# Second mixer: the groups merged inside the attention, the last projection tile by tile, the FFN begun on two of four token tiles

## Chip, cores and metric

One core of a Trainium2 chip runs the whole kernel. The metric is the device time of one execution in microseconds; the runs of the kernel before took 1180.83 to 1183.24, with a median of 1181.82. The chip's times come with one profiled execution, whose rows are quoted below.

## What is computed

A two-layer decoder trunk on 512 tokens of width 1024 in fp32. Each layer has a mixer and a gated FFN with a causal depthwise convolution, each between two RMS norms. The change touches the end of the second (odd) mixer and the start of both FFNs.

```python
def odd_mixer(h, w_in, w_out):
    cq, ck, cv, sq, sk, sv = split_cols(h @ w_in, ODD_SPLITS)
    o_dil = dilated_attention(groups(cq), groups(ck), groups(cv), slopes)  # 3 groups (window, dilation)
    o_sb = stick_breaking_attention(...)                                   # 4 heads
    return concatenate([heads_last(o_dil), heads_last(o_sb)], -1) @ w_out  # 512 x 1024
# dilated_attention, per block of 128 queries: each group g gives o_g and its log of the softmax sum;
#   wts = softmax over the groups of those logs;  o = sum over g of wts[g] * o_g
# one layer:
h = odd_mixer(rms_norm(x, pre_g), w_in, w_out);  x = x + rms_norm(h, post_g)
h = conv_ffn(rms_norm(x, ffn_pre_g), ...);       x = x + rms_norm(h, ffn_post_g)
# conv_ffn: u = causal_dwconv(h @ w_up); gate, up = split(u); (silu(gate) * up) @ w_down
```

## The kernel before

Tokens lie in four tiles of 128 (`X[0]` to `X[3]`), worked in the order `ORDER = (3, 2, 1, 0)`. The activations for the next product are held turned, 128 features by 512 tokens for each of eight feature blocks, as a high part `xh` and a low part `xl` (float32r). Every fp32 product is three float32r products, `mm3` (lines 249 to 251): high by high, high by low, low by high. Weights come through `Weights`: a load of 512 KB on SP into one of three `wraw` buffers, a cast on ScalarE (`wh`, line 71) and a subtraction on VectorE (`wl`, line 72), a few units ahead of use.

PSUM has eight banks in named groups: `BANKS = {"a": 3, "s": 2, "t": 1, "o": 1, "n": 1}`. A tile that takes a bank waits until the one that had it before has been read. The order of each engine's instructions is set when the program is built, by a scheduler that works from the order in the code and from its own estimates; within `tc.manual_schedule(engines=...)` the engines named keep the order of the code. At run time each engine works its own queue strictly in that order.

The end of the second mixer. The stick-breaking output `oS` is ready early. The dilated attention keeps two sets of results: groups 1 and 2 together (`on`, with their softmax sums in column 64 and minima in column 65; gathered by 16 small DMAs, line 1089) and group 0, worked tile by tile as score, turn (transposes), value, in `score0`, `turn0` and `value0`, with tiles of the value projection (`apv`) between them. `value0` copies its bank to `o0`. When all tiles are through, the merge weights `wt` are worked out for all tiles at once (lines 1160 to 1169). Then, for each tile, `merge(i)` weighs and adds the two results, transposes them (bank `t`) and splits them into `oh` and `ol`; `project(i, 0)` multiplies the S part of a tile (12 products with `oS`), `project(i, 1)` the merged part (12 products). The S part of a tile stands before the merged part of the tile ahead of it. `residual` follows (mean square in two halves on ScalarE, gain on VectorE, `rstd` on GpSimd, then `X` at line 238), then `normalise` (mean square of `X`, line 187, `rstd`, gain at line 200), and its `turn` (eight transposes in two groups of four at line 206, and two splits) is put off by a tile.

The FFN's first four blocks of u (`u4`, 128 features by 512 tokens each) are made specially, since the last tile is normalised late: first tokens 128 to 511 (`rest`), feature block by feature block, with the pending turn at `k == TURN`; then the last tile's 128 tokens with the weights as the moving operand (`ur`, 512 columns), copied to `us` by ScalarE and transposed into `u4` (line 367). All later blocks take 512 columns at once. This code serves both layers; the first mixer leaves one turn pending, and so does the second.

## Time and profile before

| | |
|---|---|
| median of the runs | 1181.82 us |
| profiled execution, its own time | 1183.89 us |
| its span, first to last instruction | 1182.1 us |
| TensorE busy | 1153.9 us, 98% |
| VectorE, ScalarE, GpSimd busy | 808.9, 556.7, 57.2 us |
| first product of the second mixer's projection | at 786.77 us |
| first product of the second FFN (u) | at 825.19 us |
| first u product of 512 columns there | at 850.79 us |

In rows of a timeline the columns are start, duration, engine, line, operation, result and operands, shape, count; in brackets the idle time of the engine before it and what ended it. [...] In rows of windows the columns are the stretch and its length, then the busy time of PE, PEld (weight loads), DVE, ACT and POOL, the granted TensorE clock (1.00 is full speed), the share of the DMA engines and GB/s.

### The profile page before, as it was taken

Reading aid. Unit: us, or ns where it says so; the run is one execution under the profiler, and the core shown is the slowest. Engines: PE = TensorE matmul, PEld = TensorE weight load, DVE = VectorE, ACT = ScalarE, POOL = GpSimd, SP = SyncE. Lnnn points to the kernel's source line nnn. Section 1 sums busy time; section 2 is a strip of 40 time slices with the busy share of each in tenths; the row PEclk is TensorE's granted clock in tenths of the full one; section 3 lists DMA queues with packets and bytes.
Section 4 is the critical chain, followed back from the end, with each engine's and each line's share of the span. In section 5 each row is a group of like instructions: output and inputs, shape, how many; then the busy total and the mean of one; then the engine's idle time right before and its main releaser. Section 6 shows DMA issues by size and latency. Waiting matters only on the chain. (4 is left out here: it accounts for less than half of the span.)

```text
span 1182.1 us, 14868 instructions
## 1 busy us (share of the span) xinstructions
PE 1153.9 (98%) x5520; PEld 939.7 (79%) x5520; DVE 808.9 (68%) x1401; ACT 556.7 (47%) x937; POOL 57.2 (5%) x139
## 2 busy tenths in 40 slices
PE   8999999999999999999999999997999999999997
PEld 8876866798888888888778877885988888888885
DVE  6677268557766667899863564567386665779895
ACT  5565156436343433557543464454353444435562
POOL 2100003210000000000120000002000000000001
PEclk9999999999999999999999999999999999999999
DMA  8320340033322332355635222122233233234451
GB/s 284 108 80 19 114 125 2 36 128 125 102 94 94 102 90 89 107 153 171 220 116 157 63 72 89 56 87 95 73 107 106 91 94 102 90 95 136 139 209 71
DMA packets 39048, 126.79 MB, mean 107 GB/s; under 512 B 4672, under 2 KB 6336, under 8 KB 38848
## 3 DMA queue, kind: packets, MB, share of 16 engines
q1 hardware_dynamic: 37056, 122.11, 32.2%
q10 hardware_dynamic: 1920, 3.74, 1.1%
q8 instruction: 43, 0.70, 0.2%
q14 instruction: 29, 0.24, 0.1%
HBM read 117.95 MB, written 6.29 MB: 105 GB/s over the span
## 5 line engine op out<-in xcount | busy, mean ns | idle before, releaser
L72 DVE TENSOR_TENSOR wl<-wraw,wh 128x1024 fp32r<-128x1024 f32 (+1 forms) x205 | 248.0, 1217 | 185.9 <-ACT wh L71 184.8
L71 ACT CAST wh<-wraw 128x1024 fp32r<-128x1024 f32 (+1 forms) x205 | 212.3, 1046 | 292.3 <-PE u L250 164.4
L249 PE MATMUL u<-xh,wh 128*128 128x512 f32 (+1 forms) x704 | 271.3, 386 | 0.7 <-ACT xh L170 0.7
L250 PE MATMUL u<-xl,wh 128*128 128x512 f32 (+1 forms) x704 | 271.3, 385 | 0.0
L251 PE MATMUL u<-xh,wl 128*128 128x512 f32 (+1 forms) x704 | 271.0, 385 | 0.0
L249 PEld LDWEIGHTS u<-xh,wh 128*128 128x128 f32 x704 | 132.5, 188 | 26.1 <-ACT xh L170 1.1
L250 PEld LDWEIGHTS u<-xl,wh 128*128 128x128 f32 x704 | 132.7, 189 | 25.1
L251 PEld LDWEIGHTS u<-xh,wl 128*128 128x128 f32 x704 | 132.6, 188 | 24.7
L251 PE MATMUL acc<-wh,gl 128*128 128x512 f32 x248 | 96.5, 389 | 0.0
L250 PE MATMUL acc<-wl,gh 128*128 128x512 f32 x248 | 96.5, 389 | 0.0
L249 PE MATMUL acc<-wh,gh 128*128 128x512 f32 x248 | 96.4, 390 | 0.0
L407 ACT ACTIVATE y<-u,cw 128x512 f32<-128x512 f32 x88 | 67.4, 773 | 0.9 <-PE u L367 0.9
L410 DVE SCALAR_TENSOR_TENSOR y<-u,cw,y 128x510 f32<-128x510 f32 x88 | 65.6, 747 | 2.5
L408 DVE SCALAR_TENSOR_TENSOR y<-u,cw,y 128x511 f32<-128x511 f32 x88 | 65.1, 743 | 1.8 <-ACT y L407 1.8
L412 ACT ACTIVATE y<-y 128x512 f32<-128x512 f32 x44 | 27.8, 631 | 80.2 <-DVE y L410 80.2
L249 PEld LDWEIGHTS acc<-wh,gh 128*128 128x128 f32 x248 | 46.5, 188 | 10.2 <-issue 0.6
L250 PEld LDWEIGHTS acc<-wl,gh 128*128 128x128 f32 x248 | 46.5, 188 | 9.7
L251 PEld LDWEIGHTS acc<-wh,gl 128*128 128x128 f32 x248 | 46.5, 188 | 9.6
L177 POOL TENSOR_TENSOR rv<-ms,epst 128x1 f32<-128x1 f32 x40 | 11.2, 282 | 870.0 <-ACT junk L220 804.4
L249 PE MATMUL apt<-xh,wh 128*128 128x512 f32 x128 | 51.3, 401 | 0.0
L251 PE MATMUL apt<-xh,wl 128*128 128x512 f32 x128 | 50.6, 395 | 0.0
L250 PE MATMUL apt<-xl,wh 128*128 128x512 f32 x128 | 50.5, 395 | 0.0
(295 smaller groups left out, 1937.9 us busy)
## 6 DMA issues: line engine op xcount, KB each, us to landing
wraw<-in_ffn_w_up SPq DMA_DIRECT2D x88, 512.0 KB, 3.5
wraw<-in_ffn_w_down SPq DMA_DIRECT2D x44, 512.0 KB, 3.6
wraw<-in_od_w_dqk SPq DMA_DIRECT2D x12, 512.0 KB, 3.6
wraw<-in_ffn_w_down SPq DMA_DIRECT2D x22, 256.0 KB, 2.6
wraw<-in_ev_w_dqk SPq DMA_DIRECT2D x8, 512.0 KB, 4.1
wraw<-in_ev_w_out SPq DMA_DIRECT2D x8, 512.0 KB, 3.6
spill<-X SPq DMA_DIRECT2D x8, 512.0 KB, 2.6
X<-spill SPq DMA_DIRECT2D x8, 512.0 KB, 6.7
```

The source lines that it names most:

```text
L71: self.nc.scalar.copy(h[:, :w], raw[:, :w])
L72: self.nc.vector.tensor_tensor(l[:, :w], raw[:, :w], h[:, :w].bitcast(F32), ALU.subtract)
L177: POOL.tensor_tensor(v[:, :n], ms, epst[:, :n], ALU.add)
L249: PE.matmul(o, lh, rh, start=first, stop=False, skip_group_check=more)
L250: PE.matmul(o, lh, rl, start=False, stop=False, skip_group_check=more)
L251: PE.matmul(o, ll, rh, start=False, stop=last, skip_group_check=more)
L407: ACT.activation(y[:, z], u, AF.Identity, bias=c[:, 3:4], scale=c[:, 2:3])
L408: DVE.scalar_tensor_tensor(y[:, z, 1:], u[:, :S - 1], c[:, 1:2], y[:, z, 1:], ALU.mult, ALU.add)
L410: DVE.scalar_tensor_tensor(y[:, z, 2:], u[:, :S - 2], c[:, 0:1], y[:, z, 2:], ALU.mult, ALU.add)
L412: ACT.activation(y[:, 0], y[:, 0], AF.Silu)
```

## The change

Three things. First, the merge weights and the weighted sum move into the attention, tile by tile: `turn0` works out `wt` for its tile, `value0` weighs group 0 straight out of its bank, adds the other groups, and a fourth stage, `merged`, transposes the sum and splits it into `oG`, which lies in the buffers of `cq2` to `cq5`. The copy `o0` goes. Second, the projection takes each tile whole, S terms and merged terms of one half of the columns and then of the other, in a written order for TensorE, VectorE, ScalarE and GpSimd; the banks are `s` for tiles 3 and 1 and `a` for tiles 2 and 0; a tile's turn stands between the two halves of the tile two after it, and its gain (`normed`) after the tile behind it has its `rstd`. Two turns are left for the FFN, the first of which also does the last tile's `normed`. The pool of the two `od_w_out` units (`owx`) is opened before the pool `osc`. Third, the FFN makes its first four blocks in two halves of 256 tokens: tiles 3 and 2 first, all feature blocks, with the pending turns at feature blocks 2 and 6 (at 6 alone, where one is pending), then tiles 1 and 0; the banks are `s`, `s`, `o`, `t`; `ur`, `us` and their transposes go. The first FFN is made in the same way.

```diff
 # FFN, both layers
-                rest, last = slice(P, S), slice(0, P)
                 w4 = [W.next() for _ in range(4)]
-                u4 = [bank("as"[c % 2], "u") for c in range(4)]
-                for k in range(KD):
-                    if k == TURN and pending:
-                        pending.pop(0)()
...
-                        mm3(u4[c][:, rest], wh[:, b:b + P], wl[:, b:b + P], xh[:, k, rest], xl[:, k, rest],
-                            k == 0, k == KD - 1)
-                ur = bank("o", "ur")
...
-                us = sp.tile([P, 2, S], F32, tag="y", name="us")
-                ACT.copy(us[:, 0], ur)
-                for c in range(4):
-                    PE.transpose(u4[c][:, last], us[:, 0, c * P:(c + 1) * P], ident[:])
+                u4 = [bank(tag, "u") for tag in "ssot"]
+                for half in (1, 0):
+                    t = slice(half * 2 * P, (half + 1) * 2 * P)
+                    for k in range(KD):
+                        if half and pending and k in ((2, 6) if len(pending) > 1 else (6,)):
+                            pending.pop(0)()
+                        wh, wl = w4[k // 2]
+                        for c in range(4):
+                            b = (k % 2) * S + c * P
+                            mm3(u4[c][:, t], wh[:, b:b + P], wl[:, b:b + P], xh[:, k, t], xl[:, k, t],
+                                k == 0, k == KD - 1)
 # attention, group 0: in turn0
+                            dens, nms = (st0[:, 0, i], on[:, i, :, 64]), (st0[:, 1, i], on[:, i, :, 65])
+                            DVE.tensor_tensor(mn[:], nms[0], nms[1], ALU.min)
...
+                            ACT.activation(wt[:, :, i], wt[:, :, i], AF.Exp)
...
+                            DVE.tensor_tensor(wt[:, :, i], wt[:, :, i], dn[:, 0:1].to_broadcast([P, 2, 4]), ALU.mult)
 # in value0, and the stage behind it
-                            DVE.tensor_copy(o0[:, i], o)
+                            for n in range(2):
+                                DVE.tensor_tensor(m[n][:], on[:, i, :, 0:64] if n else o,
+                                                  wt[:, n, i].unsqueeze(2).to_broadcast([P, 4, 64]), ALU.mult)
+                            DVE.tensor_tensor(m[0][:], m[0][:], m[1][:], ALU.add)
+                    def merged(i):
+                        def f(m):
+                            tp = bank("t", "tpo", 2, P)
+                            for k in range(2):
+                                PE.transpose(tp[:, k], m[:, k * P:(k + 1) * P], ident[:])
+                            q = slice(i * P, (i + 1) * P)
+                            for k in range(2):
+                                split(oG[0][k][:, q], oG[1][k][:, q], tp[:, k])
+                        return f
 # projection
-                for n, i in enumerate(ORDER):
-                    project(i, 0)
-                    merged[i] = merge(i)
-                    if n:
-                        j = ORDER[n - 1]
-                        project(j, 1)
...
+                with tc.manual_schedule(engines={PE.engine, DVE.engine, ACT.engine, POOL.engine}):
+                    for n, i in enumerate(ORDER):
+                        q = slice(i * P, (i + 1) * P)
+                        acc = [bank("as"[i % 2], "ao") for _ in range(2)]
+                        terms = [(oS[0][:, k, q], oS[1][:, k, q], *wout[2 + k]) for k in range(2)]
+                        terms += [(oG[0][k][:, q], oG[1][k][:, q], *wout[k]) for k in range(2)]
+                        t, ms = begin(sc, "t")
+                        row_product(acc, terms, True, True, (0,))
+                        part_of(t, ms, 0, acc[0], g_post)
+                        if n > 1:
+                            turns.pop(0)()
+                        row_product(acc, terms, True, True, (1,))
+                        part_of(t, ms, 1, acc[1], g_post)
+                        r = rstd(ms[:, 0:1], ms[:, 1:2])
+                        if n:
+                            normed(*norms.pop())
+                        DVE.scalar_tensor_tensor(X[i][:], t[:], r[:, 0:1], X[i][:], ALU.mult, ALU.add)
+                        norms.append((i, mean_square(X[i][:]), t))
+                        turns.append(turned(i, nx, "na", t))
+
+                def turn_next():
+                    turns[0]()
+                    normed(*norms.pop())
+
+                return nx, [turn_next, turns[1]]
```

`turned` is the part of `normalise` that makes the turn, taken out as a function of its own.

More of the change, by code (lines that the diff above doesn't have):

```diff
@@ L200, in normalise, with turned @@
                 DVE.scalar_tensor_tensor(xn[:, c], X[i][:, c], r[:, 0:1], g[:, c], ALU.mult, ALU.mult)
+            return turned(i, xnT, tags, xn)
+        def turned(i, xnT, tags, xn):
             def turn():
@@ L344, in ffn @@
                 xh, xl = xnT
-                rest, last = slice(P, S), slice(0, P)
                 w4 = [W.next() for _ in range(4)]
-                u4 = [bank("as"[c % 2], "u") for c in range(4)]
-                for k in range(KD):
-                    if k == TURN and pending:
-                        pending.pop(0)()
-                    wh, wl = w4[k // 2]
-                    for c in range(4):
-                        b = (k % 2) * S + c * P
-                        mm3(u4[c][:, rest], wh[:, b:b + P], wl[:, b:b + P], xh[:, k, rest], xl[:, k, rest],
-                            k == 0, k == KD - 1)
-                ur = bank("o", "ur")
-                for k in range(KD):
-                    wh, wl = w4[k // 2]
-                    b = slice((k % 2) * S, (k % 2) * S + S)
-                    mm3(ur, xh[:, k, last], xl[:, k, last], wh[:, b], wl[:, b], k == 0, k == KD - 1)
-                us = sp.tile([P, 2, S], F32, tag="y", name="us")
-                ACT.copy(us[:, 0], ur)
-                for c in range(4):
-                    PE.transpose(u4[c][:, last], us[:, 0, c * P:(c + 1) * P], ident[:])
+                u4 = [bank(tag, "u") for tag in "ssot"]
[9 more added lines that the diff above has]
+                                k == 0, k == KD - 1)
                 early, hold, homes = [], {}, {}
@@ L1089, in odd @@
                             nc.sync.dma_start(on[r::4, i], ob[32 * i:32 * i + 32, r])
-                    o0 = ap.tile([P, NT, 4, 64], F32, tag="ob", name="o0")
+                    oG = [[ap.tile([P, S], F32R, tag=f"cq{2 + 2 * n + k}", name="og") for k in range(2)] for n in range(2)]
                     st0 = ap.tile([P, 2, NT, 4], F32, tag="st0", name="st0")
+                    wt = ap.tile([P, 2, NT, 4], F32, tag="wt", name="wt")
                     tab0 = sb.tile([P, 4, 256], F32, tag="sh", name="tab0")
@@ L1128, in f @@
                                 (DVE.tensor_copy if u else ACT.copy)(pt[:, 2 * u:2 * u + 2, :w], tp[:, :, :w])
+                            mn = sb.tile([P, 4], F32, tag="mn", name="mn", bufs=2)
+                            dn = sb.tile([P, 2, 4], F32, tag="dn", name="dn", bufs=2)
+                            dens, nms = (st0[:, 0, i], on[:, i, :, 64]), (st0[:, 1, i], on[:, i, :, 65])
+                            DVE.tensor_tensor(mn[:], nms[0], nms[1], ALU.min)
+                            for n in range(2):
+                                DVE.tensor_tensor(wt[:, n, i], mn[:], nms[n], ALU.subtract)
+                            ACT.activation(wt[:, :, i], wt[:, :, i], AF.Exp)
+                            for n in range(2):
+                                DVE.tensor_tensor(dn[:, n], wt[:, n, i], dens[n], ALU.mult)
+                            DVE.tensor_tensor(dn[:, 0], dn[:, 0], dn[:, 1], ALU.add)
+                            DVE.reciprocal(dn[:, 0], dn[:, 0])
+                            DVE.tensor_tensor(wt[:, :, i], wt[:, :, i], dn[:, 0:1].to_broadcast([P, 2, 4]), ALU.mult)
                             return pt
@@ L1140, in f @@
                                               start=(b == 0), stop=(b == nb - 1))
-                            DVE.tensor_copy(o0[:, i], o)
+                            m = [ap.tile([P, 4, 64], F32, tag=f"ck{2 + 2 * n + i % 2}", name=f"m{n}") for n in range(2)]
+                            for n in range(2):
+                                DVE.tensor_tensor(m[n][:], on[:, i, :, 0:64] if n else o,
+                                                  wt[:, n, i].unsqueeze(2).to_broadcast([P, 4, 64]), ALU.mult)
+                            DVE.tensor_tensor(m[0][:], m[0][:], m[1][:], ALU.add)
+                            return m[0][:].rearrange("p a b -> p (a b)")
+                        return f
[7 more added lines that the diff above has]
+                                split(oG[0][k][:, q], oG[1][k][:, q], tp[:, k])
                         return f
                     tile_V = proj_V(cv)
-                    skewed([[g(i) for g in (score0, turn0, value0)] for i in ORDER],
+                    skewed([[g(i) for g in (score0, turn0, value0, merged)] for i in ORDER],
                            [lambda i=i: tile_V(i) for i in ORDER])
-                sc = es.enter_context(tc.tile_pool(name="osc", bufs=2, reuse_waits="tile"))
-                spacer(sc, 16)
-                g_post, g_next = gain("od_post_g", 0), gain("ffn_pre_g", 1)
                 wx = es.enter_context(tc.tile_pool(name="owx", bufs=2, reuse_waits="tile"))
@@ L1154, in odd @@
                 wout = [W2.next() for _ in range(2)] + [W.next() for _ in range(2)]
+                sc = es.enter_context(tc.tile_pool(name="osc", bufs=3, reuse_waits="tile"))
+                spacer(sc, 16)
+                g_post, g_next = gain("od_post_g", 0), gain("ffn_pre_g", 1)
                 nx = new_xnT()
-                mn = sc.tile([P, NT, 4], F32, tag="mn", name="mn", bufs=1)
-                wt = sc.tile([P, 2, NT, 4], F32, tag="wt", name="wt", bufs=1)
-                dn = sc.tile([P, 2, NT, 4], F32, tag="dn", name="dn", bufs=1)
@@ L1159, in odd @@
-                dens, nms = (st0[:, 0], on[:, :, :, 64]), (st0[:, 1], on[:, :, :, 65])
-                DVE.tensor_tensor(mn[:], nms[0], nms[1], ALU.min)
-                for n in range(2):
-                    DVE.tensor_tensor(wt[:, n], mn[:], nms[n], ALU.subtract)
-                ACT.activation(wt[:], wt[:], AF.Exp)
-                for n in range(2):
-                    DVE.tensor_tensor(dn[:, n], wt[:, n], dens[n], ALU.mult)
-                DVE.tensor_tensor(dn[:, 0], dn[:, 0], dn[:, 1], ALU.add)
@@ L1167, in odd @@
-                DVE.reciprocal(dn[:, 0], dn[:, 0])
-                for n in range(2):
-                    DVE.tensor_tensor(wt[:, n], wt[:, n], dn[:, 0], ALU.mult)
-                def merge(i):
-                    m = [sc.tile([P, 4, 64], F32, tag=f"m{n}", name=f"m{n}") for n in range(2)]
-                    for n in range(2):
-                        DVE.tensor_tensor(m[n][:], (o0[:, i], on[:, i, :, 0:64])[n],
-                                          wt[:, n, i].unsqueeze(2).to_broadcast([P, 4, 64]), ALU.mult)
-                    DVE.tensor_tensor(m[0][:], m[0][:], m[1][:], ALU.add)
-                    tp = bank("t", "tpo", 2, P)
-                    mf = m[0][:].rearrange("p a b -> p (a b)")
-                    for k in range(2):
-                        PE.transpose(tp[:, k], mf[:, k * P:(k + 1) * P], ident[:])
-                    oh = sc.tile([P, 2, P], F32R, tag="oh", name="oh")
-                    ol = sc.tile([P, 2, P], F32R, tag="ol", name="ol")
-                    split(oh[:], ol[:], tp[:])
-                    return oh, ol
@@ L1186, in odd @@
-                accs, merged, turns = {}, {}, []
-                def project(i, part):
-                    q = slice(i * P, (i + 1) * P)
-                    if part == 0:
-                        accs[i] = [bank("as"[i % 2 == 0], "ao") for _ in range(2)]
-                        terms = [(oS[0][:, k, q], oS[1][:, k, q], *wout[2 + k]) for k in range(2)]
-                    else:
-                        oh, ol = merged.pop(i)
-                        terms = [(oh[:, k], ol[:, k], *wout[k]) for k in range(2)]
-                    row_product(accs[i], terms, part == 0, part == 1)
@@ L1198, in odd @@
-                for n, i in enumerate(ORDER):
-                    project(i, 0)
-                    merged[i] = merge(i)
-                    if n:
-                        j = ORDER[n - 1]
-                        project(j, 1)
-                        if turns:
-                            turns.pop(0)()
-                        turns.append(normalise(j, g_next, nx, "nn", residual(j, accs.pop(j), g_post)))
-                i = ORDER[-1]
-                project(i, 1)
-                turns.pop(0)()
@@ L1210, in odd, with normed @@
-                turns.append(normalise(i, g_next, nx, "nn", residual(i, accs.pop(i), g_post)))
-                return nx, turns
+                def normed(i, r, t):
+                    for c in (slice(0, S), slice(S, D)):
+                        DVE.scalar_tensor_tensor(t[:, c], X[i][:, c], r[:, 0:1], g_next[:, c], ALU.mult, ALU.mult)
+                norms, turns = [], []
+                with tc.manual_schedule(engines={PE.engine, DVE.engine, ACT.engine, POOL.engine}):
+                    for n, i in enumerate(ORDER):
+                        q = slice(i * P, (i + 1) * P)
+                        acc = [bank("as"[i % 2], "ao") for _ in range(2)]
+                        terms = [(oS[0][:, k, q], oS[1][:, k, q], *wout[2 + k]) for k in range(2)]
+                        terms += [(oG[0][k][:, q], oG[1][k][:, q], *wout[k]) for k in range(2)]
[3 more added lines that the diff above has]
+                        if n > 1:
+                            turns.pop(0)()
+                        row_product(acc, terms, True, True, (1,))
[6 more added lines that the diff above has]
+                        turns.append(turned(i, nx, "na", t))
```

## The prediction

> **What bounds the kernel now.** I read the page's first two parts, then the table of windows in steps of 20 us, then TensorE's timeline between the second mixer's attention and the second FFN, then the other queues there.

> ```profile
> span 1182.1 us, 14868 instructions
> PE 1153.9 (98%) x5520; PEld 939.7 (79%) x5520; DVE 808.9 (68%) x1401; ACT 556.7 (47%) x937; POOL 57.2 (5%) x139
> ```

> TensorE bounds it: it idles 28 us in all. A change of order can win only that idle time, plus time at a reduced clock. The windows show where both lie together:

> ```profile
> 240.00:260.00 20.00, 20.00 (x112) 18.23 (x111) 13.80 (x16) 9.64 (x15) 2.87 (x7) 1.00 0.50 169
> 660.00:680.00 20.00, 19.19 (x79) 15.68 (x79) 11.47 (x16) 10.23 (x10) 0.10 (x1) 0.91 0.23 71
> 800.00:820.00 20.00, 16.51 (x79) 12.34 (x77) 15.90 (x23) 10.76 (x24) 4.71 (x14) 1.00 0.25 87
> 820.00:840.00 20.00, 15.90 (x82) 15.27 (x83) 8.29 (x12) 5.91 (x12) 2.93 (x7) 0.83 0.19 77
> ```

> The columns are length, PE, PEld, DVE, ACT, POOL, then the granted clock. From 800 to 840 TensorE idles 7.6 us and the clock falls to 0.83. This is the stretch that the change rewrites. Its timeline, around each wait:

> ```profile
> 796.93 0.44 PE L1180 MATMUL tpo<-ident,m 128*128 128x128 f32 x2
> 797.83 0.50 PE L249 MATMUL ao<-wh,oh 128*128 128x512 f32 x1 [0.46 <-ACT oh L170]
> ...
> 806.20 0.40 PE L249 MATMUL ao<-wh,oh 128*128 128x512 f32 x1
> 807.14 0.66 PE L206 MATMUL tp<-ident,t 128*128 128x128 f32 x4 [0.54 <-DVE t L200]
> ...
> 813.10 0.39 PE L250 MATMUL ao<-wl,oh 128*128 128x512 f32 x1
> 813.99 0.63 PE L206 MATMUL tp<-ident,t 128*128 128x128 f32 x4 [0.50 <-DVE t L200]
> ...
> 816.90 0.66 PE L206 MATMUL tp<-ident,t 128*128 128x128 f32 x4
> 823.43 1.09 PE L206 MATMUL tp<-ident,t 128*128 128x128 f32 x4 [5.88 <-DVE t L200]
> 825.19 1.33 PE L249 MATMUL u<-xh,wh 128*128 128x384 f32 x3 [0.68 <-ACT xh L170]
> ...
> 829.41 0.36 PE L250 MATMUL u<-xl,wh 128*128 128x384 f32 x1
> ```

> The large wait is the FFN: its first products need token tiles 1 to 3, and tile 1 is only then being normalised, by one serial chain:

> ```profile
> 819.09 1.27 DVE L238 SCALAR_TENSOR_TENSOR X<-t,rr,X 128x1024 f32<-128x1024 f32 x1
> 820.46 1.06 ACT L187 ACTIVATE junk<-X 128x1024 bf16<-128x1024 f32 x1 [2.28 <-DVE X L238]
> 821.95 0.55 POOL L180 TENSOR_TENSOR rr<-rv,mhalf 128x1 f32<-128x1 f32 x1
> 822.53 1.41 DVE L200 SCALAR_TENSOR_TENSOR t<-X,rr,gain 128x512 f32<-128x512 f32 x2 [2.17 <-POOL rr L180]
> ```

> **What the stretch loses.** Start-to-start times count better than idle times, since ends are modelled. The pitches:

> ```profile
> 781.43 0.28 PE L249 MATMUL apv<-wh,xh 128*128 128x256 f32 x1
> 781.55 0.28 PE L250 MATMUL apv<-wl,xh 128*128 128x256 f32 x1
> ...
> 835.53 0.33 PE L249 MATMUL u<-xh,wh 128*128 128x384 f32 x1
> 835.70 0.33 PE L250 MATMUL u<-xl,wh 128*128 128x384 f32 x1
> ...
> 845.31 0.39 PE L249 MATMUL ur<-wh,xh 128*128 128x512 f32 x1
> ...
> 850.79 0.39 PE L249 MATMUL u<-xh,wh 128*128 128x512 f32 x1
> ...
> 851.70 0.60 PE L367 MATMUL u<-ident,us 128*128 128x128 f32 x4
> 852.06 0.48 PE L250 MATMUL u<-xl,wh 128*128 128x512 f32 x1
> 852.38 0.39 PE L251 MATMUL u<-xh,wl 128*128 128x512 f32 x1
> ```

> A 256-column product takes 0.12, one of 384 takes 0.173, one of 512 takes 0.228 (24 of ur in 5.48), four transposes 0.36, and the product behind transposes 0.09 more. So the waits lose: 797.83, 0.90 less 0.22 for two transposes, 0.68; 807.14, 0.94 less 0.23, 0.71; 813.99, 0.66; 823.43, 6.53 less 0.36, 6.17. From 823.43 to 829.41 stand ten 384-column products and two groups of transposes, worth 10 x 0.173 + 2 x 0.45 = 2.63, and 5.98 us pass: 3.35 lost, mostly to the half clock. Together 11.6 us.

> **Part by part.** *FFN begin, both layers.* 96 products of 384 columns and 24 of 512 (16.6 + 5.5 = 22.1) become 192 of 256 (23.0): +0.9. The copy us and its four transposes go, -0.45. So +0.5 in each layer, +1.0. In layer 0 nothing else moves: there TensorE is busy throughout the FFN's start (20.00 of 20 us from 240 to 260), and one turn is pending in both versions. The transposes of the second mixer's tiles now stand in pairs of groups, so four switches of 0.09 go: -0.4. The new banks (s, s, o, t) are free by then, and u of the third unit waits on s behind 24 products (5.5 us), enough for two ACT and four DVE passes over u.

> *Merge in the attention.* Each tile now gets eight short DVE operations, one exp and three 256-element operations; four copies o0 go.

> ```profile
> 766.80 10.09 SPq L1089 DMA_DIRECT2D on<-ob  x16
> ...
> DMA to landing us min/median/max: 1.8/1.9/1.9
> ...
> 772.88 0.42 DVE L1111 CUSTOM_DVE_ANT_0 s<-z,tab 128x256 f32<-128x256 f32 x1 [2.78 <-PE z L1105]
> ```

> DVE, in order, now waits inside the attention for the four gathers of its tile, 16 in 10.09 us: tile 3's last starts near 768.7 and lands 1.9 later, about 770.6 to 771.1. Behind that wait stand the next scores, which TensorE does not deliver before 772.9. The 2.78 us of DVE idleness cover wait and chain; the later tiles' gathers land before their turn. I cost it at nothing; without that cover it would cost up to 1 us at tile 3.

> *What was hidden and no longer is.* Before, all S terms of tiles 3 and 2 (24 products, 5.5 us) ran ahead of the first merged term. Meanwhile ACT and DVE split three weights:

> ```profile
> 784.32 9.98 SPq L49 DMA_DIRECT2D wraw<-in_ffn_w_up  x4
> ...
> 788.06 2.94 ACT L71 CAST wh<-wraw 128x1024 fp32r<-128x1024 f32 x3
> ...
> 791.60 2.35 DVE L72 TENSOR_TENSOR wl<-wraw,wh 128x1024 fp32r<-128x1024 f32 x2
> ...
> 797.40 0.37 ACT L170 CAST oh<-tpo 128x256 fp32r<-128x256 f32 x1 [3.01 <-PE tpo L1180]
> 797.80 0.42 DVE L171 TENSOR_TENSOR ol<-tpo,oh 128x256 fp32r<-128x256 f32 x1
> ...
> wraw<-in_ffn_w_up SPq DMA_DIRECT2D x88, 512.0 KB, 3.5
> ```

> Tile by tile, only tile 3's own S terms (2.8 us with both halves, the second half standing behind) cover this. Walking the queues in the changed program's order with these durations: the merged transposes and half of the last score transposes share bank t, which has one buffer. ACT copies tile 3's first half at 787.5, then casts an FFN weight (issued 784.32, landed near 787.9, cast 1.0), then the second half; the subtraction ends near 790.0, the last score transpose follows at 790.05, its copy frees the bank at 790.9, and TensorE has lost 0.75. The two od_w_out halves of the merged rows are cast at 791.7 and 792.8 and subtracted until 794.1 and 795.4, behind the merges of tiles 1 and 0. TensorE, ready for the merged terms at 792.0, loses 0.7 (cast), 1.1 and 0.4 (subtractions). Together 2.95. The bounds: one unhidden subtraction, 1.2, and both splits unhidden, 2 x (1.0 + 1.2) = 4.4.

> *The projection and the FFN's start.* Tile 2's transposes stand after half a tile's products (2.8 us) and wait 0.3 twice for its chain of X, square, power, gain. Then the FFN needs xh of tiles 3 and 2 alone, so the 5.88 us wait for tile 1 goes. What is late next is ACT's written order: tile 2's copies stand behind tile 1's square (which waits for X1 until 815.8), a weight cast and a square, so they start near 818.5 though the transposes end at 815. TensorE, done at 817.8, waits 1.3 for xh, then 0.8 for xl, behind another weight subtraction: 2.1. Bounds: nothing, and 5.9, the wait of before; the walk's value is taken, with 0.6 for tile 2's transposes.

> New waits: 2.95 + 0.6 + 2.1 = 5.7.

> *Other queues.* On SP the spills of X1 and X0 and the table cw change places with loads of FFN weights; what they serve is cast or read only after the first u products end, 20 us later. POOL's spacer memset moves ahead of the first rstd and waits for the score transposes, done by 790.5, while rstd is first wanted near 796. Both at nothing; the cover of the first is those 23 us of products.

> *The clock.* A row shows what lowers it:

> ```profile
> 660.82 0.92 PE L961 MATMUL zp<-sq,sk 64*128 64x256 f32 x4 [0.81 <-DVE z L965]
> ```

> Around a wait of 0.81 the 660 to 680 window falls to 0.91: 0.09 x 20 / 0.5 = 3.6 us at half clock, 1.8 us of TensorE time. The new stretch from 790.2 to 795.5 loses 2.95 of 5.3 us, more. I take one such stretch, 1.5 us since part of it is idle anyway; bounds 0 and 3.0 (also at the FFN's start). [...]

> **Sum.** -11.6 - 0.4 + 1.0 + 5.7 + 1.5 = -3.8 us. The profiled execution took 1183.89 (span 1182.1 and 1.8 around it), so 1180.1 there; the median of the runs is 1181.82, 2.1 lower, so 1178.0.

> **Rivals.** *The clock stays up.* No new wait exceeds 1.4 us, against 6.2 before; the 660 row speaks against. Without the 1.5: -5.3, 1176.5.

> [...]

> *Slower: short products don't hide their weight loads.*

> ```profile
> L249 PEld LDWEIGHTS u<-xh,wh 128*128 128x128 f32 x704 | 132.5, 188 | 26.1 <-ACT xh L170 1.1
> ```

> 192 products want 192 loads of 188 ns; if nothing hid them, each would cost 0.188 instead of 0.12, 13 us per FFN and 26 in all: 1204. It decides from a pitch of 0.130 (3.8 / 384 above 0.12). Against it: the apv rows run at 0.12 with a load of the same size each. [...]

> *New waits at their upper ends.* The splits 1.4 dearer and the FFN's start as long as half of the old wait more: about -1, no change to be told. The per-queue walk speaks against.

> **How the numbers follow.** About 0.2%, 2.4 us, is what can be told from no change. Forecast 0.38, clock up 0.28, two low stretches 0.22, upper ends 0.08, loads 0.04. Two low stretches lie on the 0.2% bound, so half of them count as faster: faster 0.38 + 0.28 + 0.11, rounded to 0.78; slower 0.06, for the loads and what I have overlooked; same 0.16. The range takes in the first three cases with 0.8 below the fastest (a wait walked too long) and 1.4 above the slowest: 1175.7 to 1180.9.

> **What would show it.** In the changed profile: no wait over 2 us before the FFN's first product, which comes near 819 to 821; the second FFN's first 512-column u product near 847.4 (850.79 before, + 0.5 from the first FFN, - 11.6 - 0.4 + 0.9 + 5.7 + 1.5); three waits for ACT wh, DVE wl and bank t between 790 and 796; a pitch of 0.12 in the 256-column products; one clock dip there. Wrong would be: the FFN's start waiting over 3 us, a pitch above 0.13, DVE's merge delaying the scores, or a dip of more than two windows.

## The result and the profile after

| | before | after |
|---|---|---|
| median of the runs, beside each other | 1184.12 us | 1179.98 us |
| ratio, 95% interval | | 0.9966 [0.9952, 0.998] |
| profiled execution, its span | 1182.1 us | 1176.9 us |
| TensorE busy | 1153.9 us | 1152.7 us |
| first S product of the projection to the first u product of 512 columns ("the stretch") | 786.77 to 850.79: 64.02 us | 786.16 to 845.94: 59.78 us |

The kernel became 4.0 us faster (0.34% of 1184); 3.8 were forecast. The time forecast, 1178.0, is 2.0 us too low even so: it was counted down from the median of three runs of the kernel before, 1181.82, and over the ten runs here that kernel's median is 1184.12. The page's first lines and the windows of the stretch, after:

```profile
span 1176.9 us, 15162 instructions
PE 1152.7 (98%) x5656; PEld 942.3 (80%) x5656; DVE 811.3 (69%) x1424; ACT 557.0 (47%) x942; POOL 56.7 (5%) x139
```

```profile
780.00:800.00 20.00, 17.81 (x116) 15.04 (x115) 14.63 (x48) 9.99 (x28) 0.29 (x2) 0.91 0.34 107
800.00:820.00 20.00, 18.87 (x90) 15.05 (x88) 11.79 (x15) 9.64 (x22) 5.05 (x15) 1.00 0.20 79
820.00:840.00 20.00, 19.18 (x159) 18.97 (x160) 11.48 (x16) 6.37 (x12) 1.89 (x6) 1.00 0.24 84
```

From 800 to 840 TensorE idles 2.0 us instead of 7.6, at full clock. From 780 to 800 it now idles 2.2 us, and the clock falls to 0.91 there. The loss has become smaller and has moved to the front. TensorE's timeline, after, around every wait of the stretch:

```profile
789.88 0.44 PE L1123 MATMUL t<-ident,s 128*128 128x128 f32 x2
790.83 0.44 PE L1162 MATMUL tpo<-ident,m 128*128 128x128 f32 x2 [0.52 <-ACT pt L1124]
791.11 1.00 PE L1148 MATMUL o<-cv,pt 128*128 128x64 f32 x8
792.57 0.51 PE L253 MATMUL ao<-wh,og 128*128 128x512 f32 x1 [0.46 <-ACT wh L71]
794.22 0.79 PE L254 MATMUL ao<-wl,og 128*128 128x512 f32 x1 [1.15 <-DVE wl L72]
...
814.49 0.39 PE L255 MATMUL ao<-wh,og 128*128 128x512 f32 x1
815.16 1.23 PE L210 MATMUL tp<-ident,t 128*128 128x128 f32 x8 [0.28 <-DVE t L1183]
...
818.77 0.39 PE L255 MATMUL ao<-wh,og 128*128 128x512 f32 x1
820.16 0.74 PE L253 MATMUL u<-xh,wh 128*128 128x256 f32 x4 [1.01 <-ACT xh L170]
821.56 0.38 PE L254 MATMUL u<-xl,wh 128*128 128x256 f32 x1 [0.66 <-DVE xl L171]
```

The 5.88 us wait is gone. Six short ones stand in its place, each with the releaser that the prediction's walk of the queues gave. What holds the FFN's start is ScalarE's written order, to be read off its own timeline, after:

```profile
816.96 1.06 ACT L187 ACTIVATE junk<-X 128x1024 bf16<-128x1024 f32 x1 [3.57 <-DVE X L1204]
...
818.02 1.03 ACT L71 CAST wh<-wraw 128x1024 fp32r<-128x1024 f32 x1
818.96 0.59 ACT L224 ACTIVATE junk<-ao 128x512 bf16<-128x512 f32 x1
...
819.54 1.06 ACT L170 CAST xh<-tp 128x512 fp32r<-128x512 f32 x2
```

ScalarE stands idle for 3.57 us ahead of tile 1's square. The copies that TensorE wants (819.54) stand behind that square, a cast and another square, although their transposes were over by 816.4.

### The profile page after: what moved, and what is told of

It is laid out like the page before. It is cut to its first block, busy times and chain, and to the rows that moved or that the text cites. A ratio compares the mean times of both kernels' runs of the same rounds, so it can differ in the third digit from the quotient of the medians.

```text
span 1176.9 us, 15162 instructions
## 1 busy us (share of the span) xinstructions
PE 1152.7 (98%) x5656; PEld 942.3 (80%) x5656; DVE 811.3 (69%) x1424; ACT 557.0 (47%) x942; POOL 56.7 (5%) x139
## 5 line engine op out<-in xcount | busy, mean ns | idle before, releaser
L72 DVE TENSOR_TENSOR wl<-wraw,wh 128x1024 fp32r<-128x1024 f32 (+1 forms) x205 | 248.2, 1218 | 186.5 <-ACT wh L71 185.9
L71 ACT CAST wh<-wraw 128x1024 fp32r<-128x1024 f32 (+1 forms) x205 | 212.6, 1046 | 289.5 <-PE u L254 177.8
L253 PE MATMUL u<-xh,wh 128*128 128x512 f32 (+1 forms) x768 | 285.0, 372 | 1.0 <-ACT xh L170 1.0
L254 PE MATMUL u<-xl,wh 128*128 128x512 f32 (+1 forms) x768 | 285.2, 372 | 0.7 <-DVE xl L171 0.7
L255 PE MATMUL u<-xh,wl 128*128 128x512 f32 (+1 forms) x768 | 285.0, 371 | 0.0
L253 PEld LDWEIGHTS u<-xh,wh 128*128 128x128 f32 x768 | 144.5, 188 | 26.3 <-ACT xh L170 1.4
L254 PEld LDWEIGHTS u<-xl,wh 128*128 128x128 f32 x768 | 144.7, 188 | 25.7 <-DVE xl L171 0.9
L255 PEld LDWEIGHTS u<-xh,wl 128*128 128x128 f32 x768 | 144.7, 188 | 25.0
L253 PEld LDWEIGHTS acc<-wh,gh 128*128 128x128 f32 x248 | 46.6, 188 | 10.1 <-issue 0.5
## 6 DMA issues: line engine op xcount, KB each, us to landing
wraw<-in_ffn_w_up SPq DMA_DIRECT2D x88, 512.0 KB, 3.6
wraw<-in_ffn_w_down SPq DMA_DIRECT2D x44, 512.0 KB, 3.6
wraw<-in_od_w_dqk SPq DMA_DIRECT2D x12, 512.0 KB, 3.7
wraw<-in_ev_w_dqk SPq DMA_DIRECT2D x8, 512.0 KB, 3.7
wraw<-in_ev_w_out SPq DMA_DIRECT2D x8, 512.0 KB, 3.8
spill<-X SPq DMA_DIRECT2D x8, 512.0 KB, 2.6
X<-spill SPq DMA_DIRECT2D x8, 512.0 KB, 6.2
```

What stands on the lines that cost most here:

```text
L71: self.nc.scalar.copy(h[:, :w], raw[:, :w])
L72: self.nc.vector.tensor_tensor(l[:, :w], raw[:, :w], h[:, :w].bitcast(F32), ALU.subtract)
L253: PE.matmul(o, lh, rh, start=first, stop=False, skip_group_check=more)
L254: PE.matmul(o, lh, rl, start=False, stop=False, skip_group_check=more)
L255: PE.matmul(o, ll, rh, start=False, stop=last, skip_group_check=more)
```

## The experiments

All ratios are to the kernel before, run on the same chip in the same hour. The stretch is measured in each kernel's one profile. A ratio of 0.001 is 1.2 us. Low clock means a granted clock of 0.50; 512-column products then start 0.43 us apart (662.68 and 663.11 before), 0.23 apart otherwise.

| kernel | ratio, 95% interval | the stretch, us | low clock in it (starts) |
|---|---|---|---|
| before | 1 | 64.02 | 822.6, two windows |
| the change | 0.9966 [0.9952, 0.998] | 59.78 | 794.1 |
| e1: only the FFN's start | 0.9944 [0.9931, 0.9958] | 57.39 | none |
| e2: all but the FFN's start | 1.0 [0.9992, 1.0009] | 64.14 | 796.2; 823.5, two windows |
| e3: change, S terms ahead | 0.995 [0.9938, 0.9962] | 57.55 | none |
| e4: change, ScalarE's order | 0.9942 [0.9929, 0.9954] | 57.28 | 795.9 |
| e5: e3 and e4 | 0.9933 [0.992, 0.9946] | 54.82 | none |
| e6: change, filler products | 0.9966 [0.9954, 0.9978] | 58.93 | none |
| e7: change, first FFN as before | 0.9969 [0.9956, 0.9982] | 61.55 | 794.5; 821.8 |
| e8: e5 and e7 | 0.9922 [0.9909, 0.9934] | 56.38 | 808.5 |
| e9: e8, tile 3's gain and turn moved | 0.9905 [0.9888, 0.9922] | 53.94 | none |
| e10: e9 with the new first FFN | 0.9914 [0.9898, 0.993] | 53.94 | none |

**e1 and e2: the two halves of the change.** e1 is the kernel before with the FFN's first four blocks in two halves, and nothing else. e2 is the change with these lines as before, in both layers, and with tile 1's transposes ahead of them.

```diff
-                rest, last = slice(P, S), slice(0, P)
...
+                u4 = [bank(tag, "u") for tag in "ssot"]
+                for half in (1, 0):
...
```

> The kernel before with the FFN's new start alone; merge and projection as they were. Theory A (the gain is the FFN no longer waiting for tile 1, and the mixer's new order gives part of it back): the 6.2 us wait at tile 1's transposes and most of the 3.4 us lost to the slow clock go, the two FFN starts cost +1.0, and up to 1.5 us of new waits stand inside the FFN: 6 to 7.5 us faster than before, more than the whole change's 4. Theory B (the gain is the merge in the attention and the written order): no gain, 0 to +1 us.

> The changed kernel with the old FFN start in both layers (tile 1's turn ahead of it). Theory A: a wait for tile 1 of 4 to 6 us comes back, the waits of 790 to 796 stay: -1 to +1 us against before. Theory B: as good as the change or 1.0 better, since the short products are not paid: -4 to -5 us against before.

Waits of TensorE in e1's timeline:

```profile
799.02 0.50 PE L249 MATMUL ao<-wh,oh 128*128 128x512 f32 x1 [0.46 <-ACT oh L170]
808.34 0.66 PE L206 MATMUL tp<-ident,t 128*128 128x128 f32 x4 [0.55 <-DVE t L200]
815.19 0.63 PE L206 MATMUL tp<-ident,t 128*128 128x128 f32 x4 [0.50 <-DVE t L200]
824.64 0.63 PE L206 MATMUL tp<-ident,t 128*128 128x128 f32 x4 [0.60 <-DVE t L200]
825.82 0.38 PE L249 MATMUL u<-xh,wh 128*128 128x256 f32 x1 [0.30 <-DVE t L223]
831.44 0.63 PE L206 MATMUL tp<-ident,t 128*128 128x128 f32 x4 [0.63 <-DVE t L200]
```

and the one that decides in e2:

```profile
825.09 1.94 PE L210 MATMUL tp<-ident,t 128*128 128x128 f32 x8 [4.35 <-DVE t L1193]
```

The first three waits of e1 are those of the kernel before. Tile 1's transposes (824.64) and tile 0's (831.44) wait 0.6 us each, now inside the FFN's first half, and no window falls to the low clock. e1 gives 0.9944. e2 gives nothing: without the FFN's new start, TensorE waits 4.35 us for tile 1 after all, and the new waits take back the rest. So the gain is the FFN's start. The merge and the written order give none by themselves, and on top of the new start they seem to cost about 2.5 us: 0.9944 against 0.9966, where the intervals overlap, and a stretch of 57.39 against 59.78.

**e3 and e4: the new waits, one place each.** e3 puts the S terms of tiles 3 and 2 ahead of the first merged term, as they stood before the change. e4 puts ScalarE's copies of a tile's turn ahead of the square of the tile behind it.

```diff
 # e3
+                    for i in ORDER[:2]:
+                        S_terms(i)
...
-                        terms = [(oS[0][:, k, q], oS[1][:, k, q], *wout[2 + k]) for k in range(2)]
+                        terms = [] if ahead else [(oS[0][:, k, q], oS[1][:, k, q], *wout[2 + k]) for k in range(2)]
 # e4
-                        part_of(t, ms, 0, acc[0], g_post)
                         if n > 1:
                             turns.pop(0)()
+                        if n:
+                            j, tj = ORDER[n - 1], late.pop()
+                            norms.append((j, mean_square(X[j][:]), tj))
+                        part_of(t, ms, 0, acc[0], g_post)
...
-                        norms.append((i, mean_square(X[i][:]), t))
+                        late.append(t)
```

> The changed kernel with all S terms of tiles 3 and 2 ahead of the first merged term, the rest as it is. If the waits between 790 and 796 come from weight splits that lost their cover, the three waits (about 2.2 us by the trace) and the clock dip behind them (1.5 us) go: 2 to 3.5 us faster than the change, less what tile 3's transposes then wait, since less work stands ahead of them. If they are VectorE's throughput, the waits only move: within 0.5 us of the change.

> The changed kernel with a tile's copies and its split moved ahead of the square of the tile behind it, in ScalarE's written order. If the FFN's start waits because of that order, its first product follows the projection without the waits of 1.0 and 0.7 us: about 2 us faster than the change. If the chain of X1 is the bound, the wait moves to tile 1's transposes: within 0.5 us of the change.

In e3 no wait is left between 790 and 800, nor the low window. A new one shows 14 us later in TensorE's timeline, since the merged terms now end sooner than tile 3's normalisation:

```profile
806.67 1.32 PE L210 MATMUL tp<-ident,t 128*128 128x128 f32 x8 [1.80 <-DVE t L1183]
```

In e4 ScalarE's timeline shows the copies taken as soon as the transposes end, with the square behind:

```profile
816.50 1.07 ACT L170 CAST xh<-tp 128x512 fp32r<-128x512 f32 x2 [2.41 <-PE tp L210]
817.46 1.07 ACT L187 ACTIVATE junk<-X 128x1024 bf16<-128x1024 f32 x1
```

and TensorE goes from the projection into the FFN with no wait. The stretch is 2.2 us shorter with e3 and 2.5 with e4. The ratios, 1.9 and 2.8 us below the change's, point the same way, but both intervals overlap the change's, that of e4 only just (0.9954 and 0.9952). The waits of 1.0 and 0.7 us at the FFN's start stay in e3, and the three waits at 790 stay in e4: each edit removes its own.

**e5 and e8: together.** e5 has both edits; e8 also begins the first FFN the old way.

> The changed kernel with both repairs: S terms of tiles 3 and 2 ahead of the merged terms, and on ScalarE the copies of a tile's turn ahead of the square of the tile behind it. Each repair alone stood 1.9 and 2.8 us below the change. Theory A (the new waits are separate losses in separate places, each worth what its rows lose): the gains add, ratio near 0.9925 (1174 to 1175 us), no wait over 0.3 us from 790 to 800 nor before the FFN's first product, no clock dip in the stretch; the wait of 1.8 us for tile 3's transposes, which the ahead order alone had at 806, shrinks or stays. Rival (the chain behind the projection bounds it: what is won ahead is waited for later): no better than the ACT order alone, ratio 0.994 to 0.995, with a wait for t in the projection that takes up the difference.

> All three: S terms of tiles 3 and 2 ahead, copies ahead of the square, and the first FFN begun the old way. Theory A: the sum of the three, 0.5 us below the kernel with both repairs, ratio near 0.992 (1173.5 to 1174.5 us). Rival: as that kernel, or above it, if the first FFN's new start is a gain.

The stretch of e5 is 4.96 us shorter than the change's: the two gains add (2.2 + 2.5), as theory A says. The ratio was expected near 0.9925 and is 0.9933, with 0.9925 in its interval. The clock in e5's stretch stays up, where the change has a low window, so part of the sum is that window's. One wait is left, and it is the same in both kernels (805.13 in e5, 807.26 in e8); e5's row:

```profile
805.13 1.32 PE L210 MATMUL tp<-ident,t 128*128 128x128 f32 x8 [1.79 <-DVE t L1183]
```

Only in e8's profile does the clock fall after it; the last section comes back to that.

**e6: does idleness lower the clock?** Seven products that nobody reads stand in the first tile's waits.

```diff
+                            fill(2)
+                            lh, ll, wh, wl = terms[2]
+                            PE.matmul(acc[0], lh, wh[:, :S], start=False, stop=False)
+                            fill(5)
...
```

> The changed kernel with seven products of 512 columns that nobody reads (bank n), put into the first tile's two waits for the weight's cast and subtraction: two behind the S terms, five behind the first merged product. At 0.228 us each they take 1.6 us, which TensorE waits there anyway (0.46 + 1.15). Theory A (partly idle time lowers the clock: the waits of 0.5 to 1.2 us within 5 us cause the dip of 3.4 us at 794): the dip goes, the later products come at 0.228 instead of 0.43, and the time falls by 0.8 to 1.6 us against the change, although TensorE does more; ratio 0.9952 to 0.9960. Rival (the dip has another cause, or needs no idleness): the dip stays and the time is the same or up to 0.5 us longer; ratio 0.9965 to 0.997.

Two windows of the change, cut where the low clock begins, then two of e6, cut where windows of 3.41 us lie in its own profile (the last section has why):

```profile
790.69:794.10 3.41, 1.78 (x11) 1.33 (x11) 2.80 (x6) 2.41 (x5) 0.00 (x0) 1.00 0.51 138
794.10:797.51 3.41, 3.29 (x9) 2.60 (x10) 1.99 (x5) 0.80 (x3) 0.00 (x0) 0.50 0.65 211
```

```profile
791.82:795.23 3.41, 2.43 (x17) 1.88 (x16) 2.63 (x6) 2.25 (x5) 0.10 (x1) 1.00 0.30 54
795.23:798.64 3.41, 3.26 (x14) 2.07 (x13) 2.81 (x5) 1.18 (x4) 0.00 (x0) 1.00 0.67 195
```

With TensorE idle for 0.98 instead of 1.63 of the 3.41 us, the next window keeps the full clock, and the stretch is 0.85 us shorter although TensorE does more. Five fillers take the place of the 1.15 us wait. The two others were put wrong: they stand ahead of the last score transposes, so they only add their 0.46, and the cast's wait stays. The low window was thus worth about 0.85 + 0.46 = 1.3 us. The times don't show it: 0.9966, as the change. The profiled execution of e6 has the mean granted clock of the change's, 0.995, though its stretch has no low window: it has one at 593.9 that the change's has not.

But the fillers are not shown to be what kept the clock up. The five stand almost wholly behind the first of e6's two windows:

```profile
794.95 1.30 PE L1202 MATMUL idle<-wh,osh 128*128 128x512 f32 x5
```

That window begins 3.79 us into e6's stretch (788.03 to 791.82), and the change's 4.53 us into its own (786.16 to 790.69). Laid on e6's windows, the change's waits of 0.52, 0.46 and 1.15 would have given about 1.3 us of idleness in the first window and 0.9 in the second, without any filler. No window with so little was followed by the low clock in the stretch of any profile. So e6 doesn't decide between theory A and its rival. What ties this low window to these waits are the other kernels: the change, e2, e4 and e7, which have the three waits, all have a low window at 794 to 796, and e3, e5, e8, e9 and e10, which lack them, have none there.

**e7: the first FFN.** The change with the first FFN begun as before.

> The changed kernel with the first FFN begun the old way (384 + 128 tokens), the second the new way. The prediction costs the new start at +0.5 us in the first layer, where nothing waits for it. Theory A: 0.5 us faster than the change, ratio near 0.9962, and all later events 0.5 us earlier in the profile. Rival (the new start wins in the first layer too, by a wait or a dip that the profile before does not show, so that the FFN start alone gave 6.6 us for that reason): 0.5 to 2 us slower than the change, ratio 0.997 to 0.9985.

By the times nothing can be told: 0.9969 against the change's 0.9966, and 0.9922 against 0.9933 for e8 and e5, 0.9905 against 0.9914 for e9 and e10, which differ in the same edit. The three pairs don't agree on the direction, and the intervals of each pair overlap. The profile can tell. First u product and first of 512 columns in the first FFN, before, then after:

```profile
247.78 0.33 PE L249 MATMUL u<-xh,wh 128*128 128x384 f32 x1
...
270.90 0.39 PE L249 MATMUL u<-xh,wh 128*128 128x512 f32 x1
```

```profile
249.15 0.28 PE L253 MATMUL u<-xh,wh 128*128 128x256 f32 x1
249.26 0.28 PE L254 MATMUL u<-xl,wh 128*128 128x256 f32 x1
...
273.11 0.40 PE L253 MATMUL u<-xh,wh 128*128 128x512 f32 x1
```

23.12 us become 23.96, and in e7 they are 23.12 again. The new start costs 0.84 there, less the four transposes that stood behind: to the seventh product of 512 columns it is 25.34 us with the new start (e10) and 24.93 with the old (e9), 0.41 more. The prediction had 0.5.

**e9 and e10: the last wait.** On VectorE, tile 3's gain stands ahead of the gain of tile 2's second half (on ScalarE, tile 2's first square ahead of tile 3's); on TensorE, tile 3's transposes stand behind six S terms more.

```diff
+                        if n == 1:
+                            part_of(t, ms, 0, acc[0], g_post)
+                        if n == 2:
+                            row_product(acc, terms[:2], True, False, (1,))
+                            turns.pop(0)()
...
-                        part_of(t, ms, 1, acc[1], g_post)
+                        part_of(t, ms, 1, acc[1], g_post, (lambda: normed(*norms.pop())) if n else None)
                         r = rstd(ms[:, 0:1], ms[:, 1:2])
-                        if n:
-                            normed(*norms.pop())
```

> The kernel with all three edits (ratio 0.9922), whose only wait left in the stretch is 1.79 us for tile 3's transposes. Two edits more: tile 3's gain stands ahead of the gain of tile 2's second half on VectorE (and so for each later tile), and tile 3's transposes stand behind the six S terms of tile 1's second half. Theory A: the gain comes 1.3 us earlier, the transposes 1.4 us later in TensorE's queue, so the wait of 1.79 us goes and with it the low clock that its windows sometimes bring: 1.8 to 2.5 us less, ratio 0.990 to 0.9907, about 1171 us; in the profile no wait over 0.3 us and no clock dip between 785 and 820. Rival (what is won is waited for at tile 2's transposes or the FFN's first product, whose chain on ScalarE and VectorE is as long): ratio 0.9915 to 0.9925, with such a wait in the profile.

> As the kernel beside it, but the first FFN begun the new way, as in the change. Theory A (nothing waits for the new start in the first layer; it only costs its longer products): 0.4 to 0.5 us slower than the kernel beside it, ratio near 0.991, and in the profile 0.84 us more from the first FFN's first product to its first product of 512 columns (23.96 against 23.12 us). Rival: no slower, or faster.

In the stretch of e9 the wait of 1.79 us at tile 3's transposes is gone. One wait stands 0.1 over the bound expected, at tile 2's transposes, where the rival put it, though small (another, of 0.27, is at 827.60):

```profile
813.69 1.23 PE L210 MATMUL tp<-ident,t 128*128 128x128 f32 x8 [0.40 <-DVE t L1205]
```

The stretch is 53.94 us, 10.1 shorter than before, and the same in both kernels; against e5, which has no low window either, it is 0.9 shorter. e10's profile shows the 0.84 us expected (23.96 against 23.12). The ratio of e9, 0.9905, is the lowest, but e8, e9 and e10 can't be told apart by the times: their medians are 1172.93, 1173.05 and 1173.04 us, about 10 us below the kernel before, and their intervals overlap. So what e9's edits won is shown by the stretch alone. All three intervals lie wholly below the change's.

## Why the prediction was right, point by point

Start to start, with the prediction's pitches, on the rows of after (a row's duration overlaps the next: 256-column products of 0.28 us start 0.12 apart, at 821.90, 822.02 and 822.14):

| step | forecast, us | measured, us |
|---|---|---|
| waits of before lost | -11.6 | all four gone; 4.35 of them return in e2 |
| bank t for the merged transposes | 0.75 | 789.88 + 0.18 to 790.83: 0.77 |
| od_w_out cast | 0.7 | 791.11 + 0.85 (half of the 1.70 that 16 such products took from 786.93) to 792.57: 0.61 |
| od_w_out subtractions | 1.1 + 0.4 | 792.57 + 0.23 to 794.22: 1.42, in one |
| tile 2's transposes | 0.3 + 0.3 | 814.49 + 0.23 to 815.16: 0.44, in one |
| xh at the FFN's start | 1.3 | 818.77 + 0.23 to 820.16: 1.16 |
| xl there | 0.8 | 820.16 + 4 x 0.12 to 821.56: 0.92 |
| one low clock window | 1.5 | 1.3 (e6) |
| FFN begin, to the 512-column product | +0.9 | +0.84 (first layer) |

With the 0.4 for transposes in pairs, not measured by itself, the right column gives -11.6 - 0.4 + 2.80 + 0.44 + 2.08 + 1.3 + 0.84 = -4.5, and the stretch fell by 4.24. Walking each engine's queue in the changed program's order, with durations of before, gave every new wait, its releaser, and its size within 0.2 us. So the waits came out as forecast for the reasons given. That exactly one low window joined them was luck, as said under the rivals, and the absolute time missed by 2.0 us, by the median that it started from.

**The signs.** The FFN's first product came at 820.16 (819 to 821 forecast), no wait was over 2 us, the three early waits had the releasers named, the 256-column products run at 0.12, and one low window stands in the stretch. The first 512-column product came at 845.94, 1.5 earlier than 847.4. Of that, 0.35 lie in the stretch. The other 1.1 lie ahead of it, in no term of the sum: the low window at 662, worth an estimated 1.7 (half of 3.41), is absent from the profile after, a wait of 1.80 at 591 is 1.37 there, and against them the first FFN starts 1.4 later, behind a new low window at 12.4. These make about 0.8 of it; the rest is open.

**The merge.** Costed at nothing: from the first FFN's first product to the projection's first, 538.99 us before and 537.01 after. The absent window and the shorter wait at 591 take 2.1, and the first FFN's new start adds 0.4, so no time is left for a delay of the scores. VectorE does wait for tile 3's gathers, as forecast, and TensorE doesn't notice: from 700 to 786 it has no wait over 0.1 us after the change.

```profile
770.18 0.17 DVE L1129 TENSOR_TENSOR mn<-st,on 128x4 f32<-128x4 f32 x1 [0.68 <-DMA on<-ob]
```

**The rivals.** Unhidden weight loads are out: after, the 256-column products start 0.12 us apart, and the loads of the same rows take 192 ns each (mean, from 820 to 846). Upper ends are out by the waits. No low window (0.28) and two (0.22) were wrongly put as alternatives to the forecast's one (0.38). The profile of the change has one low window, that of e7, whose code in the stretch is the same, has two (61.55 against 59.78), and e3 has none after 1.80 us of waiting. What I priced as three different outcomes happens to one kernel from execution to execution; the median lies among them. The timed runs show the same: over the ten of the change the granted clock goes from 0.993 to 0.995, and one low window is 0.00145 of the span. The forecast's single low window was therefore one value out of several, and that the profile of the change has just one in the stretch is luck.

**A reason that was weaker than its result.** I took the price of the low clock from the 660 row, as if its wait of 0.81 had lowered it. After the change the same wait stands there and the clock stays up:

```profile
661.78 0.92 PE L956 MATMUL zp<-sq,sk 64*128 64x256 f32 x4 [0.81 <-DVE z L960]
```

**What the sum hid.** Its terms were right, but I added them up without noting that they fall into two parts of opposite sign. The FFN's start is worth 6.6 us (e1). Of the rewritten mixer's own terms, the three older waits and the pairs save 2.5, and the new waits and the low window cost some 6.6; e1 has three small waits of its own (1.5 us), so it stands only 2.4 ahead of the change in the stretch. A reader of the sum could have proposed e1, and then e4, before any run.

## What to carry to other kernels

Split a change into parts and add up each part's terms by itself: here one part held the whole gain, and repairing the order of the other made it two and a half times as large (0.9914 in e10 against 0.9966). When an order is written by hand, walk every engine's queue past each waiting instruction: a copy that another engine needs must not stand behind one that waits for a later tile (here 2.5 us of the stretch, e4). And fill the time in which weights are split with work that is ready; here the S terms of a second tile did it (2.2 us of the stretch with the low window, e3).

## What the runs showed of the hardware

```profile
803.40:806.81 3.41, 1.68 (x11) 1.35 (x12) 3.38 (x5) 1.21 (x4) 0.74 (x2) 1.00 0.00 0
806.81:810.23 3.42, 3.42 (x17) 2.80 (x16) 2.20 (x5) 2.74 (x7) 0.98 (x4) 1.00 0.37 153
```

```profile
805.09:808.50 3.41, 1.61 (x11) 1.00 (x10) 3.34 (x5) 1.25 (x4) 1.04 (x4) 1.00 0.03 10
808.50:811.91 3.41, 3.41 (x10) 2.63 (x9) 2.45 (x4) 2.42 (x6) 0.90 (x3) 0.50 0.38 154
```

and e7 at the FFN's start:

```profile
818.40:821.81 3.41, 1.72 (x10) 1.10 (x9) 3.05 (x5) 3.39 (x8) 1.66 (x4) 1.00 0.29 76
821.81:825.23 3.42, 3.42 (x18) 3.42 (x17) 3.42 (x5) 0.00 (x0) 0.00 (x1) 0.50 0.26 104
```

Before and after, the windows at full clock in which TensorE was idle for 2.51 us (9.04 after) and 3.41 us (819.21 before) were followed by a low one, as was that of 1.80 us in e8; up to 1.57 us (6.83 before) none was, but for the place at 660. Between lies either, and not by the idle time alone: 1.63 us in the change and 1.69 in e7 were followed by a low window, 1.65 before (815.79) and 1.73 in e5 were not. So the same wait cost 1.3 to 1.8 us more or not. The lower figure is e6's; the upper ones are kernels with the same code in the stretch and one low window more: 56.38 against 54.82 us (e8, e5) and 61.55 against 59.78 (e7, the change). The windows lie otherwise over the code from profile to profile (e5's begins 1.73 us ahead of tile 3's transposes, e8's 2.17), and the times spread with the clock: of 40 runs of the kernel before, made beside the experiments, the four at a granted clock of 0.995 took 1181.2 us on average and the six at 0.991 took 1185.8.

**One place falls outside this.** The place at 660, before, then in e7, each cut at its grid:

```profile
658.78:662.19 3.41, 2.46 (x12) 1.82 (x11) 3.41 (x8) 1.12 (x1) 0.10 (x1) 1.00 0.74 191
662.19:665.60 3.41, 3.41 (x9) 2.63 (x8) 2.02 (x5) 2.09 (x2) 0.00 (x0) 0.50 0.29 117
```

```profile
657.97:661.38 3.41, 2.46 (x13) 1.21 (x10) 3.22 (x5) 2.32 (x3) 0.00 (x0) 1.00 0.49 142
661.38:664.80 3.42, 3.42 (x16) 2.79 (x17) 3.24 (x8) 0.88 (x1) 0.00 (x0) 1.00 0.52 165
```

Before, one window held 0.95 us of idleness and scores on 64 of the 128 rows (L961), 2.0 us of them, and the clock fell. In e7 one window held the same 0.95 us and 2.5 us of such scores, and the clock stayed up. So neither the idle time nor these scores tell the two apart. In six of the twelve profiles (before, e1 to e4, e9) the clock falls there. The reason is open.
